# First sweep of a GLA and latent-attention layer: one float32 product in place of three float32r products, and q and k turned by VectorE and DMA

## The chip, the cores and the metric

The kernel runs on one core of one Trainium2 chip. The metric is device microseconds of one execution, taken as the median of three runs. The profile is of one more execution of the same program.

## The reference

One encoder layer over 2048 tokens of width 1024, all in float32. One input projection feeds two groups of heads, and their outputs go through one output projection, a residual and a layer norm. The change touches only the first group, a gated linear attention (GLA) with 4 heads (key width 64, value width 128), run once forwards and once backwards over chunks of tokens:

```
b = cumsum(log_a)                        # per key dimension, log_a <= 0
q_dec, k_dec = q * exp(b), k * exp(-b)
attn    = where(mask, q_dec . k_dec, 0)  # inside a chunk
o_intra = attn . v
state   = state * exp(b_last) + k_tail . v ;  o_inter = q_dec . state
o = rms_norm(o_fwd + o_bwd) * silu(gate)
```

The second group is a latent attention (MLA) with dense softmax over all 2048 keys.

## The kernel before

The program has three stages in one launch: a first sweep over 16 chunks of 128 tokens (`sweep_a`, chunk 15 down to 0, up to about 355 us of the profile), a second sweep (`sweep_c`, up to about 600 us), and the attention.

In the first sweep each chunk goes through these parts, each a generator `ga_...` of the class:

- `products`: the input projection of the chunk in three groups of columns, `ipa` tiles of PSUM. Group 0 (288 columns) holds the low-rank gates `lr` and q, group 1 (384) holds k and the first head of v, group 2 (384) the other three heads of v. Then come the gate's columns, tile `ipg` (`gate_products`, 512 columns), whose SiLU is `gate_end`, lines 1509 to 1515: three ScalarE passes and one VectorE product (`gs`). The `ipa` and `ipg` tiles share a pool of two PSUM buffers in turn: group 0 and group 2 use one, group 1 and the gate the other.
- `ga_lr`, `ga_lrT`, `ga_z`, `ga_sums`: the decay, as `E1` and `E2`, the exponentials of plus and minus the cumulated sum.
- `ga_q2`, `ga_k2`: copies q and k out of PSUM, each head's 64 columns twice side by side. `ga_q`, `ga_k`: four TensorE transposes each (`qT`, `kT`, lines 955 and 974), then times `E1` and `E2` on VectorE to `qd` and `kd`. Rows 0 to 63 of these tiles are the forward direction, rows 64 to 127 the backward one.
- `ga_kt`: `kd` transposed back (`kt`). `ga_intra`: `Ap` = k.q inside the chunk for both directions, mask, `At`. `ga_av`: `Op` = At.v. `ga_state`: `Up` = kt.v, the chunk's share of the state.

Every product of two float32 tiles is done as three float32r products of a high and a low half (`mm3`, lines 424 to 426; `hi` at line 370 makes the high half on ScalarE, `lo` at line 376 the low half on VectorE). For `Ap` the two directions stand side by side in `qbh` and `qbl`, 256 columns in which the other direction's half of the rows is zero, so that one product over 128 rows gives both. For `Op` and `Up` the high and low half of v stand side by side in `VV`, 256 columns.

The order of work: chunks 15 to 12 follow a list written out by hand (`ORDER_A`), enforced on every engine. Chunks 11 to 0 are a loop: in the step of chunk c the table `STEPS_A` puts `ga_q` and `ga_k` of the chunk before (c+1) after the fifth of the eight k-slices of group 0, `ga_kt` and `lrT` after the fifth of group 1, `z`, `cw` and `ga_intra` at the end of group 1, `ga_state` in group 2, and `ga_av` in the gate's products. Outside the hand-written list a scheduler may still move an instruction ahead where its operands are ready sooner. DMAs are issued by SyncE's queue (SP) in one order: x of a later chunk (`xaf`), and the stores of `qd`, `oi`, `Us`, `Sm` and `gs` to DRAM, which the second sweep reads. After the last chunk the weights of the second sweep (`wmr`, `wzr`) are loaded into the freed space.

Of the kernel before, what the change touches and what calls it, by code (L numbers as in the profile page):

```python
# [18 lines left out]
P = 128  # L19
# [3 lines left out]
NCH = S // P  # L23
H = 4
# [58 lines left out]
    lo=(11.99, 11.22, 11.21, 12.62, 11.98, 11.51, 10.87, 10.63),  # L83
    pv=(12.35, 12.1, 11.89, 12.65, 12.27, 12.25, 12.14, 11.45),
# [20 lines left out]
    lo=(15.35, 16.07, 20.38, 20.41, 24.45, 25.82, 33.5, 36.25),  # L105
    pv=(16.29, 16.53, 21.45, 24.62, 26.22, 30.32, 41.89, 43.83),
# [82 lines left out]
    lo=(-0.5, 0.357),  # L189
# [170 lines left out]
class K:  # L360
# [145 lines left out]
    def run(self):  # L506
        tc, nc, ins = self.tc, self.nc, self.ins
        with ExitStack() as top:
# [8 lines left out]
            self.qr_s = [[dp.tile([H, 64, QB], F32, name=f"r{p}_s{b}") for p in "hl"] for b in range(NQB)]  # L517
            self.gm_s = [dp.tile([P, H, QB], F32, name=f"gm_s{b}") for b in range(NQB)]
            self.oa_s = [dp.tile([P, H, P], F32, name=f"oa_s{c}") for c in range(NCH)]
            self.r_s = [dp.tile([1, H, QB], F32, name=f"r_s{b}") for b in range(NQB)]  # L520
            self.ob_s = [dp.tile([P, H, QB], F32, name=f"ob_s{b}") for b in range(NQB)]

# [100 lines left out]
    def sweep_a(self):  # L623
        tc, nc, ins, cp = self.tc, self.nc, self.ins, self.cp
        with ExitStack() as ctx:
# [9 lines left out]
            qbh = [wp.tile([P, H, 2, P], F32R, name=f"qbh{i}") for i in range(1)]  # L635
            qbl = [wp.tile([P, H, 2, P], F32R, name=f"qbl{i}") for i in range(1)]
# [10 lines left out]
            for t in qbh + qbl:  # L647
                nc.gpsimd.memset(t.bitcast(F32), 0.0)
            nc.vector.memset(Sb, 0.0)

            with tc.tile_pool(name="sta", bufs=1, reuse_waits="tile") as sta:
# [37 lines left out]
            cst = dict(qbh=qbh[0], qbl=qbl[0], Sb=Sb, mask=mask, rmask=rmask, wg=wg, g1=g1, tr=tr, gp=gp)  # L689
# [61 lines left out]
            with self.after(ch[i]["Ahi"]):  # L751
                self.gate_end(0, g1)
            run("state", i)
            run("av", i)
# [43 lines left out]
    def ga_k2(self, d):  # L798
        d["k2"] = d["g1"].tile([P, H, 2, 64], F32, tag="k2", name=f"k2_{d['c']}", bufs=2)
        self.hi(d["k2"], d["pt", 1][:, 0:256].rearrange("p (h o d) -> p h o d", h=H, o=1).to_broadcast([P, H, 2, 64]))  # L800
        yield

    def ga_v1(self, d):
        VV = d["VV"] = d["g1"].tile([P, H, 2, P], F32R, tag="VV", name=f"VV_{d['c']}", bufs=2)
        self.hi(VV[:, 0, 0], d["pt", 1][:, 256:384])
        yield
        self.lo(VV[:, 0, 1], d["pt", 1][:, 256:384], VV[:, 0, 0])
        yield

    def ga_v3(self, d):  # L810
        VV, pv = d["VV"], d["pt", 2][:, 0:384].rearrange("p (h d) -> p h d", h=3)
        self.hi(VV[:, 1:4, 0], pv)
        yield
        self.lo(VV[:, 1:4, 1], pv, VV[:, 1:4, 0])
        yield

    def ga_ld(self, i):
# [131 lines left out]
    def ga_q(self, d):  # L949

        nc, c = self.nc, d["c"]
        qbh, qbl = d["qbh"], d["qbl"]
        qT = d["tr"].tile([P, H, P], F32, tag="tr", name=f"qT{c}")
        for h in range(H):
            nc.tensor.transpose(qT[:, h], d["q2"][:, h].rearrange("p a d -> p (a d)"), self.ident)
        yield
        qd = self.t512(d, "qd")
# [3 lines left out]
        halves = (slice(0, 64), 0), (slice(64, 128), 1)  # L961
        for r, j in halves:
            self.hi(qbh[r, :, j], qd[r])
            yield
        for r, j in halves:
            self.lo(qbl[r, :, j], qd[r], qbh[r, :, j])
            yield

    def ga_k(self, d):

        nc, c = self.nc, d["c"]
        kT = d["tr"].tile([P, H, P], F32, tag="tr", name=f"kT{c}")
        for h in range(H):
            nc.tensor.transpose(kT[:, h], d["k2"][:, h].rearrange("p a d -> p (a d)"), self.ident)
        yield
        kd = d["kd"] = self.t512(d, "kd")
        nc.vector.tensor_tensor(kd, kT, d["E2"], ALU.mult)
        yield
        kh = d["kh"] = self.t512(d, "kh", dt=F32R)
        self.hi(kh, kd)  # L980
        yield
        kl = d["kl"] = self.t512(d, "kl", dt=F32R)
        self.lo(kl, kd, kh)
        yield

    def ga_kt(self, d):

        nc, c = self.nc, d["c"]
        kt = d["tr"].tile([P, H, P], F32, tag="tr", name=f"kt{c}")
        for h in range(H):  # L990
            nc.tensor.transpose(kt[:, h], d["kd"][:, h], self.ident)
        yield
        kth = d["kth"] = self.t512(d, "kth", dt=F32R)
        self.hi(kth, kt)
        yield
        ktl = d["ktl"] = self.t512(d, "ktl", dt=F32R)
        self.lo(ktl, kt, kth)
        yield

    def ga_intra(self, d):  # L1000

        nc, c = self.nc, d["c"]
        Ap = d["gp"].tile([P, H, 2, P], F32, tag="gp", name=f"Ap{c}")
        for h in range(H):
            self.mm3(Ap[:, h], d["kh"][:, h], d["kl"][:, h], d["qbh"][:, h], d["qbl"][:, h])
        yield
        At = self.t512(d, "At")
        nc.scalar.activation(At, Ap[:, :, 1], AF.Copy)
        yield
        nc.vector.copy_predicated(At, d["mask"][:, None, :].to_broadcast([P, H, P]), Ap[:, :, 0])  # L1010
        yield
        Ah = d["Ah"] = self.t512(d, "Ah", dt=F32R)
        d["Ahi"] = self.hi(Ah, At)
        yield
        Al = d["Al"] = self.t512(d, "Al", dt=F32R)
        self.lo(Al, At, Ah)
        yield

    def ga_av(self, d):
        nc, c = self.nc, d["c"]  # L1020
        mm = nc.tensor.matmul
        Ah, Al, VV = d["Ah"], d["Al"], d["VV"]
        Op = d["gp"].tile([P, H, 2, P], F32, tag="gp", name=f"Op{c}")
        for h in range(H):
            mm(Op[:, h], Ah[:, h], VV[:, h], start=True, stop=False)
# [4 lines left out]
        yield  # L1030
        nc.vector.tensor_tensor(oi, Op[:, :, 0], oi, ALU.add)
        self.store(c).dma_start(self.oi_s[c], oi.rearrange("p h t -> p (h t)"))
        yield

    def ga_state(self, d):

        nc, c = self.nc, d["c"]
        mm, V, G = nc.tensor.matmul, nc.vector, nc.gpsimd
        kth, ktl, VV, Sb, cw = d["kth"], d["ktl"], d["VV"], d["Sb"], self.cw[:, c]
        lo, up = slice(0, 64), slice(64, 128)  # L1040
        Up = d["gp"].tile([P, H, 2, P], F32, tag="gp", name=f"Up{c}")
        for h in range(H):
            mm(Up[:, h], kth[:, h], VV[:, h], start=True, stop=False)
            mm(Up[:, h, 0], ktl[:, h], VV[:, h, 0], start=False, stop=True)
        yield
        Us = self.t512(d, "Us")
        nc.scalar.activation(Us, Up[:, :, 1], AF.Copy)
        yield
        V.tensor_tensor(Us, Up[:, :, 0], Us, ALU.add)  # L1049
        yield  # L1050
        G.tensor_tensor(Us, Us, cw[:, 1, :, None].to_broadcast([P, H, P]), ALU.mult)  # L1051
        self.store(c).dma_start(self.su_s[c][lo], Us.rearrange("p h t -> p (h t)")[lo])
        yield
        if d["i"] > 2:
            yield from self.ga_bst(d)
        if c > 0:
            G.tensor_tensor(Sb[up], Sb[up], Us[up], ALU.add)
        yield

    def ga_bst(self, d):  # L1060
# [987 lines left out]
```

## Time and profile before

| | us |
|---|---|
| median of 3 runs (1295.48 to 1295.51) | 1295.5 |
| profiled execution, its own time | 1295.28 |
| its span in the profile | 1293.4 |
| TensorE busy in the span | 1273.7 |
| VectorE / ScalarE / GpSimd busy | 962.8 / 816.2 / 786.1 |

In a row of the timeline the columns are start, duration, engine, line, operation, output <- inputs, shapes and count. Matmuls are pipelined: a row's duration is its latency, and what it costs TensorE is the distance from its start to the start of the next row. PEld is the loading of a matmul's weights, which runs beside the matmul ahead of it. A float32 matmul that is not a transpose shows as two rows of PE and two of PEld, a float32r one as one of each. The windows give, for each stretch, the busy time of PE, PEld, VectorE (DVE), ScalarE (ACT) and GpSimd (POOL), the granted clock of TensorE, the DMA engines' busy share, and GB/s.

### The profile page before, as it was taken

The page shows a single profiled execution, that of the slowest core. Times are in us where ns is not written, and L with a number is a line of the kernel's source. Part 1 is how long each engine was busy: PE and PEld are TensorE (multiplying, and loading weights), DVE is VectorE, ACT ScalarE, POOL GpSimd, SP SyncE. Part 2 cuts the span into 40 slices and gives each one's busy share as a digit, 9 for nine tenths or more (in the row PEclk, how much of TensorE's full clock was granted, in tenths as well). Part 3 has the DMA queues.
Part 4 walks back from the last instruction along what each step waited for, and adds up shares of the span by engine and source line. Part 5 has one row for each costly group of instructions (what it writes and reads, how often), then busy time and mean ns, then how long its engine had stood idle before and what let it go on. Part 6 is the DMA issues. An engine that isn't in the chain of part 4 may idle for free.

```text
span 1293.4 us, 19959 instructions
## 1 busy us (share of the span) xinstructions
PE 1273.7 (98%) x7082; PEld 1127.9 (87%) x7082; DVE 962.8 (74%) x1706; ACT 816.2 (63%) x1334; POOL 786.1 (61%) x494
## 2 busy tenths in 40 slices
PE   8999999999999999999999999999999999999997
PEld 7999999999989999999788888888888888888886
DVE  7966675656675455554898888888888889469997
ACT  7765656566676656665688888888888888511110
POOL 0143333242458666762298888889999999944441
PEclk9999999999999999999999999999999999999999
DMA  8222313132475555665401111122223110366652
GB/s 294 66 92 56 93 53 94 50 86 62 143 261 174 194 197 179 200 208 174 128 1 41 42 42 41 42 58 63 61 72 103 46 41 9 123 214 201 214 193 98
DMA packets 105795, 145.81 MB, mean 113 GB/s; under 512 B 16630, under 2 KB 59262, under 8 KB 105696
## 3 DMA queue, kind: packets, MB, share of 16 engines
q1 hardware_dynamic: 97632, 142.41, 35.3%
q0 software_dynamic: 672, 2.10, 0.4%
q8 instruction: 56, 0.92, 0.3%
q10 hardware_dynamic: 7392, 0.03, 0.3%
q14 instruction: 43, 0.35, 0.1%
HBM read 94.14 MB, written 50.36 MB: 112 GB/s over the span
## 4 chain that ended last, share of the span: by engine, by line
PE 85%; DVE 4%; issue 2%; POOL 2%; ACT 1%; DMA 1%; SPq 0%; DVEq 0%; POOLq 0%
PE pz L1222 6%; PE ipm L1293 5%; PE o L424 4%; PE o L425 4%; PE o L426 4%; PE pS L1554 4%; PE pS L1556 4%; PE pS L1557 4%; PE pS L1555 4%; PE pS L1558 4%; PE ipa L424 4%; PE ipa L426 4%; PE ipa L425 4%; PE ipg L424 2%; PE ipg L425 2%
## 5 line engine op out<-in xcount | busy, mean ns | idle before, releaser
L376 POOL TENSOR_TENSOR pl<-s,ph 128x1024 fp32r<-128x1024 f32 x128 | 306.1, 2409 | 57.5 <-ACT ph L370 53.6
L1576 DVE TENSOR_TENSOR rm<-pS,rm 128x512 f32<-128x512 f32 x210 | 144.8, 690 | 35.8 <-ACT s L1563 30.5
L1563 ACT ACTIVATE s<-pS 128x1024 f32<-128x1024 f32 x128 | 131.3, 1026 | 61.0 <-PE pS L1558 50.8
L1600 DVE TENSOR_TENSOR s<-s,mb 128x1024 f32<-128x1024 f32 x128 | 151.2, 1213 | 9.2 <-PE mb L1594 9.0
L1051 POOL TENSOR_TENSOR Us<-Us,cw 128x512 f32<-128x512 f32 x16 | 20.0, 1247 | 226.3 <-DVE Us L1049 187.8
L370 ACT ACTIVATE ph<-s 128x1024 fp32r<-128x1024 f32 x128 | 135.1, 1057 | 17.4 <-PE o L426 16.6
L1604 ACT ACTIVATE s<-s 128x1024 f32<-128x1024 f32 x128 | 131.4, 1050 | 11.9 <-DVE s L1600 11.9
L424 PE MATMUL ipa<-wah,xah 128*128 128x384 f32 (+1 forms) x384 | 129.0, 336 | 5.4 <-ACT wah L370 5.4
L425 PE MATMUL ipa<-wal,xah 128*128 128x384 f32 (+1 forms) x384 | 124.3, 324 | 0.6 <-DVE wal L376 0.5
L426 PE MATMUL ipa<-wah,xal 128*128 128x384 f32 (+1 forms) x384 | 124.4, 324 | 0.0
L1554 PE MATMUL pS<-qh,ckvT_h 128*128 128x512 f32 x256 | 102.6, 401 | 0.8 <-DVE rm L1576 0.4
L424 PE MATMUL o<-ph,vh 128*128 128x512 f32 x256 | 101.0, 395 | 0.0
L426 PE MATMUL o<-ph,vl 128*128 128x512 f32 x256 | 99.8, 390 | 0.0
L1556 PE MATMUL pS<-qh,ckvT_l 128*128 128x512 f32 x256 | 99.8, 390 | 0.0
L1557 PE MATMUL pS<-rh,krs 128*128 128x512 f32 x256 | 99.8, 390 | 0.0
L1558 PE MATMUL pS<-rl,krs 128*128 128x512 f32 x256 | 99.7, 389 | 0.0
L1555 PE MATMUL pS<-ql,ckvT_h 128*128 128x512 f32 x256 | 99.7, 389 | 0.0
L425 PE MATMUL o<-pl,vh 128*128 128x512 f32 x256 | 99.7, 389 | 0.0
L1627 DVE TENSOR_TENSOR ap<-ap,s 128x512 f32<-128x512 f32 x120 | 83.1, 692 | 2.6 <-ACT s L1604 0.7
L376 POOL TENSOR_TENSOR ol<-of,oh 128x512 fp32r<-128x512 f32 x32 | 42.9, 1342 | 63.8 <-ACT oh L370 63.8
L424 PEld LDWEIGHTS ipa<-wah,xah 128*128 128x128 f32 x384 | 72.8, 190 | 6.6 <-ACT wah L370 5.6
L425 PEld LDWEIGHTS ipa<-wal,xah 128*128 128x128 f32 x384 | 72.8, 190 | 1.8 <-DVE wal L376 1.3
(325 smaller groups left out, 3838.8 us busy)
## 6 DMA issues: line engine op xcount, KB each, us to landing
xcf<-xT_dram SPq DMA_DIRECT2D x16, 512.0 KB, 5.6
xr<-x_dram SPq DMA_DIRECT2D x16, 512.0 KB, 5.5
out_dram<-rr SPq DMA_DIRECT2D x32, 256.0 KB, 2.1
xaf<-xT_dram SPq DMA_DIRECT2D x14, 512.0 KB, 4.2
oib<-oi_s SPq DMA_DIRECT2D x16, 256.0 KB, 4.3
qdb<-qd_s SPq DMA_DIRECT2D x16, 256.0 KB, 5.1
SU<-su_s SPq DMA_DIRECT2D x16, 256.0 KB, 4.9
ub<-u_s SPq DMA_DIRECT2D x16, 256.0 KB, 4.2
```

The lines of the kernel that those rows point to most:

```text
L370: return nc.scalar.activation(dst, src, AF.Copy).ins
L376: return e.tensor_tensor(dst, src, hi.bitcast(F32), ALU.subtract).ins
L424: mm(out, ah, bh, start=start, stop=False)
L425: mm(out, ah, bl, start=False, stop=False)
L426: mm(out, al, bh, start=False, stop=stop)
L1554: mm(ps[:, e], kh, qh, start=True, stop=False)
L1555: mm(ps[:, e], kh, ql, start=False, stop=False)
L1556: mm(ps[:, e], kl, qh, start=False, stop=False)
L1557: mm(ps[:, e], kr, rh, start=False, stop=False)
L1558: mm(ps[:, e], kr, rl, start=False, stop=True)
L1576: V.tensor_tensor(d["rm"], src[:, e], d["rm"], ALU.max)
L1600: V.tensor_tensor(s, s, d["mb"][:, None, :].to_broadcast([P, 2, QB]), ALU.subtract)
```

## The change

It has two parts, both in the first sweep.

For all 16 chunks the high and low halves behind `Ap`, `Op` and `Up` go. Each is a plain float32 product, on `qd`, `kd`, `At`, `kt` and `V` as they are. `Ap` becomes eight products over 64 rows each, by turns over rows 0 to 63 and 64 to 127, and the two directions go to different PSUM banks (`Ap` is now `[P, 2, H, P]`). `Us` is scaled straight out of PSUM by VectorE instead of by GpSimd.

For chunks 11 to 0 (steps i from 4 to 15) `ga_q2`/`ga_k2` and the TensorE transposes go. `turn` lets VectorE transpose q (or k) within 32x32 blocks, and four DMAs from SP write it to a DRAM tile in whole transposed order, in runs of 32 float32 (128 bytes). `turned` reads it back with two DMAs, once into rows 0 to 63 and once into rows 64 to 127. `qx` follows group 0; `ql` (the reading of q) and `kx` follow group 1; `kl` (the reading of k) follows group 2.

```
+    def turn(self, d, n, src):
+        t = d["g1"].tile([P, H, 2, 32], F32, tag=f"{n}x", name=f"{n}x_{d['c']}")
+        self.nc.vector.transpose(t.rearrange("p h a t -> p (h a t)"), src)
+        dst = self.qk_s["qk".index(n)][d["c"]].rearrange("(a r) h (b t) -> b r h a t", a=2, b=4)
+        for b in range(4):
+            self.nc.sync.dma_start(dst[b], t[32 * b:32 * b + 32])
+
+    def turned(self, d, n):
+        t = d[f"{n}T"] = self.t512(d, f"{n}2", bufs=2)
+        for r in (slice(0, 64), slice(64, 128)):
+            self.nc.sync.dma_start(t[r], self.qk_s["qk".index(n)][d["c"]])
...
-            for n in ((("lr", "q2"), ("k2", "v1"), ("v3",)) if i else (("lr",), ("q2", "k2", "v1"), ("v3",)))[g]:
+            for n in ((("lr", "qx"), ("ql", "kx", "v1"), ("kl", "v3")) if i else (("lr",), ("q2", "k2", "v1"), ("v3",)))[g]:
...
     def ga_q(self, d):
-        for h in range(H):
-            nc.tensor.transpose(qT[:, h], d["q2"][:, h].rearrange("p a d -> p (a d)"), self.ident)
+        qT = d.get("qT")
+        if qT is None:
...
-        for r, j in halves:
-            self.hi(qbh[r, :, j], qd[r])
-        for r, j in halves:
-            self.lo(qbl[r, :, j], qd[r], qbh[r, :, j])
...
     def ga_k(self, d):
-        kh = d["kh"] = self.t512(d, "kh", dt=F32R)
-        self.hi(kh, kd)
-        kl = d["kl"] = self.t512(d, "kl", dt=F32R)
-        self.lo(kl, kd, kh)
...
     def ga_kt(self, d):
-        self.hi(kth, kt)
-        self.lo(ktl, kt, kth)
+        d["kt"] = self.t512(d, "kt")
+        self.hi(d["kt"], kt)
...
     def ga_intra(self, d):
-        Ap = d["gp"].tile([P, H, 2, P], F32, tag="gp", name=f"Ap{c}")
+        Ap = d["gp"].tile([P, 2, H, P], F32, tag="gp", name=f"Ap{c}")
         for h in range(H):
-            self.mm3(Ap[:, h], d["kh"][:, h], d["kl"][:, h], d["qbh"][:, h], d["qbl"][:, h])
+            for j, r in enumerate((slice(0, 64), slice(64, 128))):
+                nc.tensor.matmul(Ap[:, j, h], d["kd"][r, h], d["qd"][r, h], start=True, stop=True)
...
-        d["Ahi"] = self.hi(Ah, At)
-        self.lo(Al, At, Ah)
...
     def ga_av(self, d):
-            mm(Op[:, h], Ah[:, h], VV[:, h], start=True, stop=False)
-            mm(Op[:, h, 0], Al[:, h], VV[:, h, 0], start=False, stop=True)
+            nc.tensor.matmul(Op[:, h], d["At"][:, h], d["V"][:, h], start=True, stop=True)
-        nc.scalar.activation(oi, Op[:, :, 1], AF.Copy)
-        nc.vector.tensor_tensor(oi, Op[:, :, 0], oi, ALU.add)
+        nc.scalar.activation(oi, Op, AF.Copy)
...
     def ga_state(self, d):
-            mm(Up[:, h], kth[:, h], VV[:, h], start=True, stop=False)
-            mm(Up[:, h, 0], ktl[:, h], VV[:, h, 0], start=False, stop=True)
+            nc.tensor.matmul(Up[:, h], d["kt"][:, h], d["V"][:, h], start=True, stop=True)
-        nc.scalar.activation(Us, Up[:, :, 1], AF.Copy)
-        V.tensor_tensor(Us, Up[:, :, 0], Us, ALU.add)
-        G.tensor_tensor(Us, Us, cw[:, 1, :, None].to_broadcast([P, H, P]), ALU.mult)
+        nc.vector.tensor_tensor(Us, Up, cw[:, 1, :, None].to_broadcast([P, H, P]), ALU.mult)
```

`ga_v1` and `ga_v3` lose their low halves (`VV` becomes `V`, float32), and the tiles `qbh` and `qbl` with their memsets go.

More of the change, by code (lines that the diff above doesn't have):

```diff
@@ L519, in run @@
             self.oa_s = [dp.tile([P, H, P], F32, name=f"oa_s{c}") for c in range(NCH)]
+            self.qk_s = [[dp.tile([64, H, P], F32, name=f"{n}_s{c}") for c in range(NCH)] for n in ("qx", "kx")]
             self.r_s = [dp.tile([1, H, QB], F32, name=f"r_s{b}") for b in range(NQB)]
@@ L634, in sweep_a @@
             lrs = [wp.tile([P, 98], F32R, name=f"lr{i}") for i in range(2)]
-            qbh = [wp.tile([P, H, 2, P], F32R, name=f"qbh{i}") for i in range(1)]
-            qbl = [wp.tile([P, H, 2, P], F32R, name=f"qbl{i}") for i in range(1)]
             Sb = wp.tile([P, H, P], F32, name="Sb")
@@ L646, in sweep_a @@
                 nc.vector.memset(t[:, 96:98].bitcast(F32), 1.0)
-            for t in qbh + qbl:
-                nc.gpsimd.memset(t.bitcast(F32), 0.0)
             nc.vector.memset(Sb, 0.0)
@@ L687, in sweep_a @@
             g1 = ctx.enter_context(tc.tile_pool(name="g1", bufs=1))
-            cst = dict(qbh=qbh[0], qbl=qbl[0], Sb=Sb, mask=mask, rmask=rmask, wg=wg, g1=g1, tr=tr, gp=gp)
+            cst = dict(Sb=Sb, mask=mask, rmask=rmask, wg=wg, g1=g1, tr=tr, gp=gp)
             rope = self.rope_angles(pos_i, pos_f, invf, hpi)
@@ L750, in sweep_a @@
             run("intra", i)
-            with self.after(ch[i]["Ahi"]):
+            with self.after(ch[i]["Aset"]):
                 self.gate_end(0, g1)
@@ L801, in ga_k2, with ga_qx, ga_kx, ga_ql @@
         yield
+    def turn(self, d, n, src):
[8 more added lines that the diff above has]
+            self.nc.sync.dma_start(t[r], self.qk_s["qk".index(n)][d["c"]])
+    def ga_qx(self, d):
+        self.turn(d, "q", d["pt", 0][:, 32:288])
+        yield
+    def ga_kx(self, d):
+        self.turn(d, "k", d["pt", 1][:, 0:256])
+        yield
+    def ga_ql(self, d):
+        self.turned(d, "q")
+        yield
+    def ga_kl(self, d):
+        self.turned(d, "k")
+        yield
     def ga_v1(self, d):
[L804 to L807, printed above, removed]
+        d["V"] = self.t512(d, "V", bufs=2)
+        self.hi(d["V"][:, 0], d["pt", 1][:, 256:384])
         yield
     def ga_v3(self, d):
[L811 to L814, printed above, removed]
+        self.hi(d["V"][:, 1:4], d["pt", 2][:, 0:384].rearrange("p (h d) -> p h d", h=3))
         yield
@@ L951, in ga_q @@
         nc, c = self.nc, d["c"]
-        qbh, qbl = d["qbh"], d["qbl"]
-        qT = d["tr"].tile([P, H, P], F32, tag="tr", name=f"qT{c}")
-        for h in range(H):
-            nc.tensor.transpose(qT[:, h], d["q2"][:, h].rearrange("p a d -> p (a d)"), self.ident)
-        yield
-        qd = self.t512(d, "qd")
+        qT = d.get("qT")
+        if qT is None:
+            qT = d["tr"].tile([P, H, P], F32, tag="tr", name=f"qT{c}")
+            for h in range(H):
+                nc.tensor.transpose(qT[:, h], d["q2"][:, h].rearrange("p a d -> p (a d)"), self.ident)
+            yield
+        qd = d["qd"] = self.t512(d, "qd")
         nc.vector.scalar_tensor_tensor(qd, qT, 0.125, d["E1"], ALU.mult, ALU.mult)
@@ L960, in ga_q @@
         yield
-        halves = (slice(0, 64), 0), (slice(64, 128), 1)
-        for r, j in halves:
-            self.hi(qbh[r, :, j], qd[r])
-            yield
-        for r, j in halves:
-            self.lo(qbl[r, :, j], qd[r], qbh[r, :, j])
-            yield
     def ga_k(self, d):
         nc, c = self.nc, d["c"]
[L972 to L975, printed above, removed]
+        kT = d.get("kT")
+        if kT is None:
+            kT = d["tr"].tile([P, H, P], F32, tag="tr", name=f"kT{c}")
+            for h in range(H):
+                nc.tensor.transpose(kT[:, h], d["k2"][:, h].rearrange("p a d -> p (a d)"), self.ident)
+            yield
         kd = d["kd"] = self.t512(d, "kd")
         nc.vector.tensor_tensor(kd, kT, d["E2"], ALU.mult)
-        yield
-        kh = d["kh"] = self.t512(d, "kh", dt=F32R)
-        self.hi(kh, kd)
-        yield
-        kl = d["kl"] = self.t512(d, "kl", dt=F32R)
-        self.lo(kl, kd, kh)
         yield
@@ L992, in ga_kt @@
         yield
-        kth = d["kth"] = self.t512(d, "kth", dt=F32R)
-        self.hi(kth, kt)
-        yield
-        ktl = d["ktl"] = self.t512(d, "ktl", dt=F32R)
-        self.lo(ktl, kt, kth)
+        d["kt"] = self.t512(d, "kt")
+        self.hi(d["kt"], kt)
         yield
@@ L1020, in ga_av @@
         nc, c = self.nc, d["c"]
[L1021 to L1023 removed]
+        Op = d["gp"].tile([P, 2, H, P], F32, tag="gp", name=f"Op{c}")[:, 0]
         for h in range(H):
[L1025 to L1026 removed]
+            nc.tensor.matmul(Op[:, h], d["At"][:, h], d["V"][:, h], start=True, stop=True)
         yield
         oi = self.t512(d, "oi", bufs=2)
[L1029 to L1031 removed]
+        nc.scalar.activation(oi, Op, AF.Copy)
         self.store(c).dma_start(self.oi_s[c], oi.rearrange("p h t -> p (h t)"))
@@ L1037, in ga_state @@
         nc, c = self.nc, d["c"]
-        mm, V, G = nc.tensor.matmul, nc.vector, nc.gpsimd
-        kth, ktl, VV, Sb, cw = d["kth"], d["ktl"], d["VV"], d["Sb"], self.cw[:, c]
+        Sb, cw = d["Sb"], self.cw[:, c]
         lo, up = slice(0, 64), slice(64, 128)
-        Up = d["gp"].tile([P, H, 2, P], F32, tag="gp", name=f"Up{c}")
+        Up = d["gp"].tile([P, 2, H, P], F32, tag="gp", name=f"Up{c}")[:, 0]
         for h in range(H):
-            mm(Up[:, h], kth[:, h], VV[:, h], start=True, stop=False)
-            mm(Up[:, h, 0], ktl[:, h], VV[:, h, 0], start=False, stop=True)
+            nc.tensor.matmul(Up[:, h], d["kt"][:, h], d["V"][:, h], start=True, stop=True)
         yield
         Us = self.t512(d, "Us")
-        nc.scalar.activation(Us, Up[:, :, 1], AF.Copy)
+        nc.vector.tensor_tensor(Us, Up, cw[:, 1, :, None].to_broadcast([P, H, P]), ALU.mult)
+        self.store(c).dma_start(self.su_s[c][lo], Us.rearrange("p h t -> p (h t)")[lo])
         yield
-        V.tensor_tensor(Us, Up[:, :, 0], Us, ALU.add)
         yield
-        G.tensor_tensor(Us, Us, cw[:, 1, :, None].to_broadcast([P, H, P]), ALU.mult)
-        self.store(c).dma_start(self.su_s[c][lo], Us.rearrange("p h t -> p (h t)")[lo])
         yield
@@ L1056, in ga_state @@
         if c > 0:
-            G.tensor_tensor(Sb[up], Sb[up], Us[up], ALU.add)
+            nc.gpsimd.tensor_tensor(Sb[up], Sb[up], Us[up], ALU.add)
         yield
```

10 lines of the change are left out of this document (3 added, 7 removed).

## The prediction

> **What bounds the kernel now.** I read the page's busy shares first, then the windows, then who waited for whom on TensorE inside the first sweep, and then one step of a chunk row by row.
>
> ```profile
> span 1293.4 us, 19959 instructions
> PE 1273.7 (98%) x7082; PEld 1127.9 (87%) x7082; DVE 962.8 (74%) x1706; ACT 816.2 (63%) x1334; POOL 786.1 (61%) x494
> ...
> 150.00:200.00 50.00, 50.00 (x324) 47.78 (x323) 30.89 (x56) 30.60 (x59) 18.37 (x13) 1.00 0.27 74
> ...
> PE Up L1044 <- DVE ktl L376: 0.4, 1, 0.4
> ...
> PE Ap L426 <- DVE kl L376: 0.3, 1, 0.3
> ...
> PE Op L1025 <- ACT Ah L370: 0.4, 1, 0.4
> ```
>
> TensorE is busy in 50.00 of these 50 us at a granted clock of 1.00, VectorE in 30.89, ScalarE in 30.60, GpSimd in 18.37; DMA takes 0.27. The three waits of TensorE that have to do with this change come to 1.1 us over 16 chunks. So what is taken from VectorE, ScalarE and GpSimd in the first sweep is worth those 1.1 us at most, what is taken from TensorE counts, and the new DMAs cost nothing until TensorE waits for them. The later stages keep their instructions; they start earlier or later with the sweep.
>
> One step in the timeline, with the places that change:
>
> ```profile
> 239.11 0.39 PE L426 MATMUL ipg<-wgh,xal 128*128 128x512 f32 x1
> 239.34 0.29 PE L424 MATMUL ipa<-wah,xah 128*128 128x288 f32 x1
> 239.47 0.29 PE L425 MATMUL ipa<-wal,xah 128*128 128x288 f32 x1
> ...
> 241.31 0.60 PE L955 MATMUL qT<-ident,q 128*128 128x128 f32 x4
> 241.75 0.60 PE L974 MATMUL kT<-ident,k 128*128 128x128 f32 x4
> 242.10 0.38 PE L424 MATMUL ipa<-wah,xah 128*128 128x288 f32 x1
> 242.32 0.29 PE L425 MATMUL ipa<-wal,xah 128*128 128x288 f32 x1
> ...
> 243.38 0.35 PE L424 MATMUL ipa<-wah,xah 128*128 128x384 f32 x1
> ```
>
> **Transposes of q and k.** From the first qT (241.31) to the second projection row behind kT (242.32) is 1.01 us; two projection rows stand 0.13 us apart, so the eight transposes cost 0.88 us of TensorE. They go in 12 chunks: **-10.6 us**.
>
> **What is late next.** In the changed program as built, `kt` no longer waits for the middle of group 1: two of its four transposes stand ahead of group 1, and group 1 has to wait until VectorE has read the gate out of the same PSUM buffer (`gs`). That chain:
>
> ```profile
> 239.31 1.06 ACT L370 ACTIVATE xah<-xaf 128x1024 fp32r<-128x1024 f32 x1 [1.98 <-PE ipg L425]
> 240.28 0.58 ACT L1509 ACTIVATE gs<-ipg 128x512 f32<-128x512 f32 x1
> ...
> 241.56 0.63 ACT L1513 ACTIVATE gs<-gs 128x512 f32<-128x512 f32 x1
> ...
> 242.56 0.68 DVE L1515 TENSOR_TENSOR gs<-ipg,gs 128x512 f32<-128x512 f32 x1
> ...
> 223.79 0.60 PE L991 MATMUL kt<-ident,kd 128*128 128x128 f32 x4
> 224.22 0.27 PE L891 MATMUL lrT<-ident,lr 128*98 128x128 f32 x1
> ```
>
> Today `gs` ends at 243.24 and group 1 starts at 243.38, unhindered. ScalarE keeps xah and its three passes in this order, so `gs` can start at 242.25 at the earliest (ScalarE ends at 242.19) and end at 242.93; with 0.1 us allowed for the hand-over, group 1 may start at about 243.03. TensorE would be there at 243.38 - 0.88 + 0.3 (two transposes of `kt`, 0.43/2, and the change into and out of them) = 242.80. So 0.2 us of the 0.88 turn into a wait, and the moved half of `kt` gives back 0.22 of its 0.3. That is 0.28 us in each of 11 steps (chunk 0 has no step behind it): **+3.1 us**; bounds 0, if the silu chain gets that much earlier too, and +6.3, if group 1 keeps today's 0.14 us behind `gs` and nothing of `kt` is given back.
>
> **The float32 products.** The trace has one plain float32 product, `pabs` of the second sweep: eight products of 128x128x128, 16 rows.
>
> ```profile
> 372.43 1.95 PE L1186 MATMUL pabs<-wkr,wqT 128*128 128x128 f32 x16
> 374.13 0.36 PE L1222 MATMUL pz<-xch,wzh 128*128 128x256 f32 x1
> 374.33 0.28 PE L1222 MATMUL pz<-xcl,wzh 128*128 128x256 f32 x1
> ...
> 372.23 1.96 PEld L1186 LDWEIGHTS pabs<-wkr,wqT 128*128 128x128 f32 x16
> 374.10 0.19 PEld L1222 LDWEIGHTS pz<-xch,wzh 128*128 128x128 f32 x1
> ...
> 226.32 0.33 PE L424 MATMUL Ap<-qbh,kh 128*128 128x256 f32 x1
> ...
> 227.78 0.35 PE L424 MATMUL ipa<-wah,xah 128*128 128x384 f32 x1
> ...
> 229.89 0.28 PE L1043 MATMUL Up<-VV,kth 128*128 128x256 f32 x1
> ...
> 230.75 0.39 PE L424 MATMUL ipa<-wah,xah 128*128 128x384 f32 x1
> ...
> 235.68 0.28 PE L1025 MATMUL Op<-VV,Ah 128*128 128x256 f32 x1
> ...
> 236.53 0.45 PE L424 MATMUL ipg<-wgh,xah 128*128 128x512 f32 x1
> ```
>
> Eight take 1.70 us by the matmuls (372.43 to 374.13) and 1.87 by the weight loads (372.23 to 374.10): 0.21 to 0.23 us each. `Up` now takes 0.86 us, `Op` 0.85; four float32 products each are 0.85 to 0.94. Taken at +0.01 for each of 32: **+0.3 us** (bounds 0 and +2.7).
>
> `Ap` now takes 1.46 us (226.32 to 227.78). The new eight products have 64 rows each, by turns in the lower and the upper half of the array, from disjoint partitions into different banks. No row of this trace has a product over half the rows. If they run one behind the other they cost what `pabs` costs, up to 1.87 us; if each two run side by side, half of 1.70, 0.85. Neither row is nearer, and a partial overlap (weights loaded one after the other, products side by side) lies between; I take the middle, 1.35 us: -0.11 in 16 chunks, **-1.8 us** (bounds -9.8 and +6.6). The Trainium skill says two things here. TensorE: Matmul & The Clock Gate, Part 3, has matmuls in different row groups start about 4 ns apart, which would give the lower bound. TensorEngine Tiling (Array Packing), Key Properties, says "Changing tiling mode (not just tile) drains the TensorE", which speaks against the change; no row here can show either.
>
> **Waits and the end of the sweep.** The three waits above go with `kl`, `ktl` and `Ah`: **-1.1 us** (bounds -1.1 and 0). In chunk 0 no gate of a next step covers the way of k: from the end of group 1 to `kt` there are only group 2, `Op` and 18 gate products; I put **+0.5 us** there (0 to 1). Behind it the splitting of the second sweep's weights on VectorE loses the low halves queued ahead of it, so it is not later than today.
>
> **VectorE, ScalarE, GpSimd** lose the halves, and GpSimd the scaling of `Us`, which VectorE does in place of an addition of the same shape. VectorE gains two block transposes of 128x256, an operation that the trace lacks; between the split of 128x128 and a product of 128x512:
>
> ```profile
> 226.92 0.29 DVE L376 TENSOR_TENSOR VV<-ipa,VV 128x128 fp32r<-128x128 f32 x1 [1.18 <-ACT VV L370]
> ...
> 234.26 0.68 DVE L1049 TENSOR_TENSOR Us<-Up,Us 128x512 f32<-128x512 f32 x1
> ```
>
> 0.29 to 0.68 us each, 0.45 taken; hidden, as VectorE is idle 19 of 50 us.
>
> **The way through DRAM.** Twelve DMAs more in each step on SP. Rows:
>
> ```profile
> 220.69 0.34 SPq L490 DMA_DIRECT2D xaf<-xT_dram  x1
> ...
> 221.59 0.38 SPq L855 DMA_DIRECT2D u_s<-gs  x1
> 236.19 0.45 SPq L1052 DMA_DIRECT2D su_s<-Us  x1
> ...
> 225.93 0.56 PE L903 MATMUL z<-lrTs,wg 98*128 98x128 f32 x4
> ...
> gm_s<-gm SPq DMA_DIRECT2D x8, 512.0 KB, 3.6
> oa_s<-oT SPq DMA_DIRECT2D x16, 256.0 KB, 2.1
> su_s<-Us SPq DMA_DIRECT2D x14, 128.0 KB, 2.2
> ```
>
> SP issues two in 0.90 us (220.69 to 221.59, one row between) and is free from 222 to 236. One q or k is 4 x 256 runs of 128 bytes, 64 packets on each of 16 engines. The nearest price: `gm_s` is 512 runs of 1 KB (32 an engine) and lands in 3.6 us, `oa_s` is 128 runs of 2 KB (8 an engine) in 2.1: 1.5/24 = 62 ns a packet, which a shorter run should not exceed; the lower end is nothing beyond the 2.1.
> At 62 ns, in the clock of the step above (k leaves PSUM from 225.93, `kt` comes at the end of the next group 0, 242.5): q's writes queue behind the loads and stores issued from 220.7 on and land by 230. SP issues the first write of k at 226.9, then waits at the reading of q until 230 and so keeps the other three writes of k waiting; these go out until 232.3 and land by 237. The reading of k waits for them; its second half stands behind the store of `Us`, ready at 234.9. Issued by 238, landed by 241 (2.2 in the row of `su_s`, 3 allowed), `kd` (0.68, as `gs`) done by 241.7. That is 0.8 us ahead of `kt`, and at half the price 3 us or more. So **0 us** on TensorE; behind this wait on VectorE stand `gs` and the next `lr` and `qx`, which would then be late too.
>
> **Sum** against the profiled execution (1295.28 us; span 1293.4 and 1.9 around it; the median of the runs is 0.2 above): -10.6 + 3.1 + 0.3 - 1.8 - 1.1 + 0.5 = -9.6, so 1285.7, and on the scale of the median **1286 us**. With `Ap` fully side by side 1278; with `Ap` at 1.65 us 1291: the forecast's own range, chance 0.6.
>
> **Rivals.** *The 64-row products run singly* (0.22): `Ap` at 1.87 gives 1294. If the array has to run empty at each change between 128 and 64 rows, it costs the end of a row that is otherwise overlapped, 0.27 us long less the 0.11 at which transposes follow each other, twice in 16 chunks: +5, and 1299 (0.06 of the 0.22; this is the rule of TensorEngine Tiling in the Trainium skill). For it: the weight loads of `pabs` are as dense as its matmuls, so nothing is left to overlap if loads stay in one line. Against it: the halves share neither partitions nor banks. A measurement of this kernel tells 0.2% from no change, 2.6 us (1292.9 to 1298.1), so most of this rival is "same".
>
> *The way through DRAM comes late* (0.13), slower. Place: `kd` on VectorE, ahead of `kt` and `gs`. It decides from about 70 ns a packet: 64 packets of q and 48 of k stand in one line, so 7 ns more use up the 0.8 us. At 90 ns `kt` waits (112 x 28 ns) - 0.8 = 2.3 us in 11 steps, +25.6, and the time is 1311; at 80 ns 1299. For it: no store in the trace has runs this short. The Trainium skill (DMA: Bandwidth & Descriptors, Specifications) says that below 512 B a write becomes a read-modify-write; no run here shows it. Against it: the sweep's DMA share is 0.27.
>
> A remainder (0.05) is for a cost not seen, above all in the hand-ordered chunks 15 to 12 and at the change to the second sweep. That the change doesn't do what it says is no case: the eight transposes are TensorE rows that go.
>
> **Chances and range.** Faster 0.6 + 0.03 of the single products = 0.63; same 0.13 (singly, without the array running empty); slower 0.24 (the rest). 1277 to 1301 leaves out some 0.05 below and, above, the DRAM case beyond 80 ns and part of the remainder, some 0.13.
>
> **What would show it.** In the changed profile: no `qT`, `kT` after 100 us; group 1 waiting some 0.2 us for `gs` in each step; `Ap` from first row to next `ipa` 0.85 to 1.87 us; `kd` ending before group 0 does; TensorE's share of the windows still full. Wrong if TensorE waits for `kd` in every step (the DRAM way), if `Ap` takes more than 1.9 us, or if the stretch behind 355 us grows.

## The result, and the profile after

| | before, us | after, us |
|---|---|---|
| median (5 runs each) | 1295.51 | 1288.98 |
| range of the runs | 1295.48 to 1296.32 | 1288.48 to 1290.23 |
| span of the profile | 1293.4 | 1287.2 |

The ratio is 0.9947, with a 95% interval of 0.9936 to 0.9958: 6.5 us faster, where 9.5 were forecast. From the page of the changed kernel, the window of the sweep that the prediction showed, and the three longest of the waits of TensorE that are new (us in total, times, longest):

```profile
PE 1262.9 (98%) x7050; PEld 1110.6 (86%) x7050; DVE 912.8 (71%) x1602; ACT 755.5 (59%) x1230; POOL 765.9 (60%) x476
...
150.00:200.00 50.00, 49.60 (x321) 46.27 (x321) 25.69 (x42) 19.54 (x43) 14.43 (x9) 1.00 0.44 114
...
PE ipm L1287 <- DVE xcl L376: 1.4, 1, 1.4
PE kt L1002 <- DVE kd L994: 1.2, 1, 1.2
PE pS L1548 <- ACT s L1557: 1.0, 1, 1.0
```

TensorE lost 10.8 us of work (1273.7 to 1262.9) and the span 6.2. In the window TensorE is no longer full (49.60 of 50.00) and DMA has gone from 0.27 to 0.44. None of the three waits stood in the trace of before.

One step of the sweep, TensorE's timeline of the changed kernel (start, duration, line, operation, count):

```profile
215.44 0.29 PE L426 MATMUL ipa<-wah,xal 128*128 128x288 f32 x1
215.57 0.38 PE L1002 MATMUL kt<-ident,kd 128*128 128x128 f32 x2
216.08 0.45 PE L424 MATMUL ipa<-wah,xah 128*128 128x384 f32 x1
216.37 0.34 PE L425 MATMUL ipa<-wal,xah 128*128 128x384 f32 x1
...
218.82 0.38 PE L1002 MATMUL kt<-ident,kd 128*128 128x128 f32 x2
219.04 0.27 PE L912 MATMUL lrT<-ident,lr 128*98 128x128 f32 x1
...
220.73 0.56 PE L924 MATMUL z<-lrTs,wg 98*128 98x128 f32 x4
221.22 1.16 PE L1014 MATMUL Ap<-qd,kd 64*128 64x128 f32 x16
222.31 0.44 PE L424 MATMUL ipa<-wah,xah 128*128 128x384 f32 x1
222.59 0.33 PE L425 MATMUL ipa<-wal,xah 128*128 128x384 f32 x1
...
240.53 0.27 PE L912 MATMUL lrT<-ident,lr 128*98 128x128 f32 x1
```

From `lrT` to `lrT` a step is 21.49 us (219.04 to 240.53), where before's are mostly 22.21 to 22.24: some 0.70 us in each step. Of the eleven steps of chunks 10 to 0, nine lie at 21.46 to 21.52; the two from 262.05 to 306.53 take 22.21 and 22.27, and before they took 24.90 and 20.26. Between 215.44 and 222.59 no `qT` or `kT` is left; the two halves of `kt` stand at 215.57 and 218.82; `Ap` takes 1.09 us to the start of the next row.

The sweep's lead was 9.3 us when the second sweep began (first `ipm` at 358.23 instead of 367.56), 7.7 us at its first `pz` (366.44 instead of 374.13), 6.4 us at the last `pS` of the attention (1081.29 instead of 1087.68). So the sum of -9.6 was right up to the end of the first sweep, though by errors that cancel (see below), and some 3 us were given back behind it.

### The profile page after: what moved, and what is told of

It is laid out like the page before. It is cut to its first block, busy times and chain, and to the rows that moved or that the text cites. A ratio compares the mean times of both kernels' runs of the same rounds, so it can differ in the third digit from the quotient of the medians.

```text
span 1287.2 us, 19847 instructions
## 1 busy us (share of the span) xinstructions
PE 1262.9 (98%) x7050; PEld 1110.6 (86%) x7050; DVE 912.8 (71%) x1602; ACT 755.5 (59%) x1230; POOL 765.9 (60%) x476
## 4 chain that ended last, share of the span: by engine, by line
PE 81%; DMA 5%; DVE 4%; ACT 3%; issue 3%; POOL 2%; SPq 2%; DVEq 0%; ACTq 0%; POOLq 0%
PE pz L1216 6%; PE ipm L1287 5%; PE o L424 4%; PE o L425 4%; PE o L426 4%; PE pS L1548 4%; PE pS L1550 4%; PE pS L1551 4%; PE pS L1552 4%; PE pS L1549 4%; PE ipa L424 4%; PE ipa L426 3%; PE ipa L425 3%; PE ipg L425 2%; PE ipg L424 2%
## 5 line engine op out<-in xcount | busy, mean ns | idle before, releaser
L1051 POOL TENSOR_TENSOR Sb<-Sb,Us 64x512 f32<-64x512 f32 x15 | 21.5, 1434 | 188.0 <-ACT E L961 133.7
```

## The experiments

All were compared with the kernel before, which stood at 1296.0 us beside `f32_only`, `turn_only`, `ap_by_half` and `xah_late` and at 1295.28 us beside the other four. Each trace is of one run. For `split_late` (1296.19 us), `ap_by_half` (1298.58) and `xah_late` (1290.93) that run is 1.7 to 3 us above the median given here.

### Each half of the change alone

*Float32 products alone* (`f32_only`): q and k are turned by TensorE in all chunks, as before.

```
-            for n in ((("lr", "qx"), ("ql", "kx", "v1"), ("kl", "v3")) if i else (("lr",), ("q2", "k2", "v1"), ("v3",)))[g]:
+            for n in ((("lr", "q2"), ("k2", "v1"), ("v3",)) if i else (("lr",), ("q2", "k2", "v1"), ("v3",)))[g]:
```

> Only the float32 products; q and k of every chunk are still transposed by TensorE. Theory (both parts pay, the products by the pairs of 64 rows): a step between two lrT transposes shrinks by 0.37 us in Ap less 0.2 for the two changes of 64 and 128 rows, and 0.05 in Up and Op, so 0.2 of 22.2 us in each step, some 3.5 us over 16 chunks and up to 1 us of waits: 1291 to 1292.5. Rival (the products are worth nothing, all of the gain is the transposes): 1295.5 within 1 us.

Measured: 1293.27 us, ratio 0.998 [0.9971, 0.9989], so 2.7 us less than before, and 0.8 us outside the range that I expected. Its steps are 22.04 to 22.08 us, on average 0.15 less than before. At the first `ipm` it is 3.75 us ahead of before (363.81 instead of 367.56), at the first `pz` 2.7 (371.41 instead of 374.13): between them TensorE waits 0.8 us for `xcl`, a wait that comes back in the changed kernel.

*Turning through DRAM alone* (`turn_only`): the products stay split in halves, and `Us` stays with GpSimd. What the kernel keeps of before:

```
         Ap = d["gp"].tile([P, H, 2, P], F32, tag="gp", name=f"Ap{c}")
         for h in range(H):
             self.mm3(Ap[:, h], d["kh"][:, h], d["kl"][:, h], d["qbh"][:, h], d["qbl"][:, h])
```

> Only the turning of q and k by VectorE and DMA in chunks 11 to 0; the products stay three float32r products. Theory: a step loses the eight transposes (0.88 us) and gets back 0.4 of it around kt and the start of group 1, which waits for gs: 21.7 instead of 22.2 us a step, 12 steps, less some 1 to 2 us at the change to the second sweep: 1290.5 to 1292. Rival (the transposes are worth all of the gain): 1289. Rival (the DRAM way alone costs more than it brings, since kd and its halves now stand on VectorE ahead of gs): 1295 or more.

Measured: 1350.04 us, ratio 1.042 [1.0406, 1.0435]. My expectation was wrong by over 50 us. The second rival has the direction, and its reason (`kd` and its halves stand on VectorE ahead of `gs`) points at the order of work; its first words blame the way through DRAM. The trace tells the two apart. TensorE's largest wait, then one step on ScalarE, VectorE, SP and TensorE:

```profile
PE ipa L424 <- DVE gs L1549: 41.2, 11, 4.2
...
239.09 1.28 ACT L370 ACTIVATE qbh<-qd 64x512 fp32r<-64x512 f32 x2 [0.97 <-DVE qd L990]
244.43 0.63 ACT L370 ACTIVATE kh<-kd 128x512 fp32r<-128x512 f32 x1 [4.06 <-DVE kd L1011]
...
245.44 1.05 ACT L370 ACTIVATE xah<-xaf 128x1024 fp32r<-128x1024 f32 x1
...
240.69 2.98 DVE L376 TENSOR_TENSOR qbl<-qd,qbh 64x512 fp32r<-64x512 f32 x2
243.70 0.69 DVE L1011 TENSOR_TENSOR kd<-k,E 128x512 f32<-128x512 f32 x1
...
234.80 1.12 SPq L815 DMA_DIRECT2D k<-kx_s  x2
...
249.08 0.44 PE L424 MATMUL ipa<-wah,xah 128*128 128x384 f32 x1 [4.13 <-DVE gs L1549]
```

k's reading went out at 234.80, nine microseconds before `kd`, and `kd` has no wait in brackets behind it: it is late because VectorE does two `qbl` first, which take 2.98 us. On ScalarE `kh` waits 4.06 us for `kd`, and behind `kh` are queued `xah` and the gate's passes, which in the kernel before stood ahead of it. So `gs`, and with it group 1, comes four microseconds late. If this reading holds, the cause is the order on VectorE and ScalarE and not the DRAM way.

*The same with the splitting put behind the gate* (`split_late`): one edit against `turn_only`.

```
     def ga_kt(self, d):
...
             nc.tensor.transpose(kt[:, h], d["kd"][:, h], self.ident)
         yield
+        if d["i"] > 3:
+            with self.after(*self.gs_done):
+                for _ in self.split_q(d):
+                    pass
+                for _ in self.split_k(d):
+                    pass
```

(`split_q` and `split_k` are the four lines each that make `qbh`, `qbl`, `kh`, `kl`; they leave `ga_q` and `ga_k`. `gs_done` is the gate's last ScalarE pass and its VectorE product.)

> The kernel with the turning through DRAM and float32r products (the one of 1350 us), with one change: from chunk 4 of the order on, the splitting of qd and kd in halves (qbh, kh on ScalarE, qbl, kl on VectorE) is put behind the gate's activations and gs of the step, not ahead of them. Theory: the way through DRAM is in time there too, and the 4.2 us that TensorE waited for gs in each step came of kh standing ahead of xah and the gate on ScalarE, and kd behind two qbl of 1.5 us on VectorE; then the steps fall from 26 to 21.5 to 22.0 us and the time to 1288 to 1293 us. Rival: q and k through DRAM take VectorE and SP so much time with the halves there that kd is late wherever the halves stand: steps above 23.5 us and a time above 1310.

Measured: 1293.24 us, ratio 0.9987 [0.9976, 0.9998]. The steps are mostly 21.66 us, in the range of the theory and 0.55 below before; the time is 0.24 us above its range. The 57 us between the two kernels are shown to be the place of the splitting; what its part on ScalarE and its part on VectorE cost apart is not. Two places keep it from gaining more. One is the step from 286.23 to 310.89, which takes 24.66 us with two waits of TensorE, 1.01 for `kd` and 0.76 for `gs`. The other is chunk 0, where the splitting still stands ahead:

```profile
345.10 3.14 DVE L376 TENSOR_TENSOR qbl<-qd,qbh 64x512 fp32r<-64x512 f32 x2 [0.23 <-ACT qbh L370]
...
349.61 1.12 PE L1037 MATMUL kt<-ident,kd 128*128 128x128 f32 x4 [2.91 <-DVE kd L1017]
```

With this wait of 2.91 us the granted clock falls, and is 0.50 from 349 to 355.

In the steps the two halves of the change add up: -0.15 (products) and -0.55 (turning), against -0.70 together.

### The 64-row products

*`Ap` by halves* (`ap_by_half`): the changed kernel, with the four products of rows 0 to 63 first and those of rows 64 to 127 behind them, not by turns.

```
-        for h in range(H):
-            for j, r in enumerate((slice(0, 64), slice(64, 128))):
+        for j, r in enumerate((slice(0, 64), slice(64, 128))):
+            for h in range(H):
```

> The changed kernel, with the eight 64-row products of Ap in another order: four in the lower half of the array, then four in the upper half, instead of by turns. Theory (two products in different halves run side by side): Ap goes from 1.09 us to the price of products one behind the other, 1.7 to 1.9 us, +0.6 to +0.8 in 16 chunks, 1298 to 1301. Rival (64-row products are cheaper by themselves, by their fewer rows): Ap stays at 1.1 us and the time at 1289.

Measured: 1296.78 us, ratio 1.0004 [0.9995, 1.0013], 7.8 us above the changed kernel by the medians and 7.4 by the ratios; I had expected at least 1298. TensorE's timeline:

```profile
226.41 1.71 PE L1014 MATMUL Ap<-qd,kd 64*128 64x128 f32 x16
228.04 0.44 PE L424 MATMUL ipa<-wah,xah 128*128 128x384 f32 x1
```

1.63 us to the next row, where the turns take 1.09. In 16 chunks 0.54 us are 8.6 us. By turns the trace's rows start in pairs, 7 ns apart within a pair and 0.11 us from pair to pair; by halves most of them start singly, 0.11 us apart, and only a few around the change of half pair up. So products over different halves of the rows run side by side where they stand next to each other in the order: the same 16 rows, the same operands. The order of two loops is worth about as much as the whole change brought.

### The wait of group 1 for the gate

*`xah` late* (`xah_late`): the changed kernel, with the splitting of the next x on ScalarE put behind the gate's three passes.

```
-        self.hi(xh[:, :, 0], xf)
+        with self.after(*([self.gs_act] if i > 4 else [])):
+            self.hi(xh[:, :, 0], xf)
```

> The changed kernel, with the high half of the next x (xah, 1.06 us on ScalarE) put behind the three SiLU passes instead of ahead of them. Theory (group 1 waits for the SiLU chain): gs ends 1 us earlier, group 1 follows group 0 without a wait, a step falls from 21.5 to about 21.1 us and the time by 11 x 0.4 = 4.4 to about 1284.6, less what the second sweep's DMAs hold back. Rival (TensorE is held by kt, which waits for kd from DRAM): no change of the step, 1289.

Measured: 1289.22 us, ratio 0.9948 [0.9935, 0.996]: nothing gained over the change. Yet the steps are 21.11 us, 0.39 less, as expected. One step loses it again. TensorE's timeline at its two ends, a wait, VectorE, and the window from the end of that wait to the end of the step (the last three columns are granted clock, DMA share, GB/s):

```profile
280.70 0.32 PE L913 MATMUL lrT<-ident,lr 128*98 128x128 f32 x1 [0.25 <-DVE lr L376]
...
307.37 0.42 PE L913 MATMUL lrT<-ident,lr 128*98 128x128 f32 x1
...
PE ipa L424 <- DVE gs L1510: 3.4, 1, 3.4
...
299.48 1.42 DVE L995 TENSOR_TENSOR kd<-k,E 128x512 f32<-128x512 f32 x1 [7.51 <-DMA k<-kx_s]
300.82 0.68 DVE L1510 TENSOR_TENSOR gs<-ipg,gs 128x512 f32<-128x512 f32 x1
...
301.56:307.37 5.81, 5.81 (x19) 5.71 (x20) 0.39 (x2) 0.00 (x0) 0.00 (x0) 0.50 0.63 158
```

The step from 280.70 to 307.37 takes 26.67 us instead of after's 22.27. There k's reading went out at 294.11, behind two stores of the step and a load of x in SP's order, and came after 299.4; behind `kd` stands `gs`. TensorE waits 3.43 us for it, and at a granted clock of 0.50 the 5.81 us behind the wait cost some 2.9 more. This is the DRAM rival's place, in one step of twelve; the late start of the reading comes of SP's order.

*Sf cleared by GpSimd* (`sf_pool`): the changed kernel, with one instruction on another engine.

```
-            self.nc.vector.memset(Sf, 0.0)
+            self.nc.gpsimd.memset(Sf, 0.0)
```

The reason, from the changed kernel's VectorE and TensorE timelines at the end of the sweep:

```profile
355.93 0.48 DVE L1117 MEMSET Sf<- 64x512 f32 x1 [3.14 <-DMA oi_s<-oi]
...
358.90 2.35 DVE L376 TENSOR_TENSOR xcl<-xcf,xch 128x1024 fp32r<-128x1024 f32 x2
...
360.17 0.47 PE L1287 MATMUL ipm<-wmh,xcl 128*128 128x448 f32 x1 [1.38 <-DVE xcl L376]
```

> The changed kernel with one instruction moved: Sf, the tile of the second sweep's state, is set to zero by GpSimd instead of VectorE. Theory: in the changed kernel the clearing of Sf waits for the store of oi, which lands late in the stretch with full DMA engines behind 340 us, and VectorE's splitting of xcl behind it makes TensorE wait 1.4 us ahead of ipm. With the clearing off VectorE that wait goes: 1287.6 us (1287.0 to 1288.3). Rival: the transfers of that stretch themselves come 1.4 us too late, since the first sweep now ends earlier; then TensorE waits as long for the next of them, and the time stays at 1289.

Measured: 1286.7 us, ratio 0.9928 [0.9916, 0.9941]. The first `pz` comes 1.0 us earlier than in the changed kernel (365.4), and the wait of `ipm` is gone. From the first `ipm` to the first `pz` TensorE takes 6.57 us, as before, where the changed kernel takes 8.21. The first `ipm` itself comes 0.6 us later (358.82), since in this run `kt` of chunk 0 waits 0.61 us for `kd`. By the medians the gain over the changed kernel is 2.3 us, where 1.4 was expected, and the time lies just below the range that I gave. The runs (1285.14 to 1287.26) lie below all of the changed kernel's, so the rival, 1289, is out; whether the gain is 1.4 or 2.3 they don't tell.

*Both* (`best`): `xah` late in steps 5 to 12 only, and Sf on GpSimd.

```
+        with self.after(*([self.gs_act] if 4 < i < 13 else [])):
...
+            self.nc.gpsimd.memset(Sf, 0.0)
```

> The changed kernel with two edits: in steps 5 to 12 the splitting of the next x (xah, ScalarE) goes behind the gate's three activations, and Sf is cleared by GpSimd. Theory: the wait of group 1 for gs costs 0.39 us a step, as the steps of 21.11 instead of 21.50 us in the kernel with xah late in all steps show, and that kernel lost its gain only in one later step, at k's reading behind the stores of the step. Without that step: 8 x 0.39 = 3.1 and 1.4 from Sf, 1284.5 us (1283.5 to 1286). Rival: whatever the steps gain is given back before the second sweep, since the end of the first sweep waits for transfers: 1288 to 1289.

Measured: 1282.72 us, ratio 0.9911 [0.9897, 0.9924]: 12.6 us below before and some 6 below the changed kernel, and lower than the range of the theory. It is clear of `xah_late`; against `sf_pool` the intervals overlap. Seven steps, from the `lrT` at 89.72 to the one at 237.53, take 21.11 or 21.12 us each, and the first `ipm` comes at 354.95.

### How much the DRAM way has to spare

*Each short write twice* (`twice`): a second tile in DRAM takes a copy that nothing reads.

```
+            self.nc.sync.dma_start(twin[b], t[32 * b:32 * b + 32])
             self.nc.sync.dma_start(dst[b], t[32 * b:32 * b + 32])
```

> The changed kernel, with each of the 96 writes of 128-byte runs (qx_s, kx_s) also sent to a second place in DRAM that nothing reads, ahead of the real one: twice the short packets and twice the issues on SP. Theory: kd is 3.3 us ahead of kt in the changed kernel, and the writes cost what SP takes to issue them (0.64 us each, 5.1 us more a step), so k's reading goes out 4 to 5 us later, kd comes 1 to 2 us too late for kt, and 12 steps cost 12 to 25 us: 1301 to 1314. By the 62 ns a packet of the prediction (64 packets more for q and for k on each engine, 8 us) it would be above 1335. Rival: the slack is larger than it looks, and the time stays below 1292.

Measured: 1310.71 us, ratio 1.012 [1.0106, 1.0133]. TensorE's waits, and in one step SP's queue and VectorE:

```profile
PE kt L1005 <- DVE kd L997: 13.9, 8, 3.0
PE ipm L1290 <- DVE xcl L376: 5.9, 1, 5.9
...
215.59 0.61 SPq L809 DMA_DIRECT2D kx_s<-kx  x1
...
220.90 0.33 SPq L984 DMA_DIRECT2D qd_s<-qd  x1
...
221.81 1.12 SPq L814 DMA_DIRECT2D k<-kx_s  x2
...
225.28 0.69 DVE L997 TENSOR_TENSOR kd<-k,E 128x512 f32<-128x512 f32 x1 [4.40 <-DMA k<-kx_s]
```

`kt` now waits for `kd`, 1.7 us in each of eight steps, 13.9 together, within the 12 to 25 that the theory gave for this place. The other large part is at the change to the second sweep, where `ipm` waits 5.9 us for `xcl` (1.4 in the changed kernel). A write holds SP for 0.61 us. But the last of them goes out at 215.59 and k's reading only at 221.81: with the writes later, the store of `qd` has come to stand ahead of the reading in SP's queue (220.90), and it waits for VectorE. So the theory's mechanism, issues that push the reading back, is only half of it; the other half is what the reading then stands behind. The 62 ns a packet of the prediction would have made the time above 1335 us; the measured time is far below.

## Why the prediction was right or wrong

**The likeliest case came in, at 1289.0 instead of 1286.0.** By its terms:

- *Transposes*, -0.88 us a step: no `qT` or `kT` row is left. Right.
- *Group 1 behind `gs`*, +0.28 a step: the changed kernel shows 0.93 us from 215.44 to 216.37, with half of `kt` and the wait in it; without them three such rows stand 0.13 and 0.17 us apart, so 0.63 is theirs; the other half takes 0.22 less than all of `kt` did. That makes +0.40, and `xah_late` takes 0.39 of it away. The mechanism was right; the term was 0.12 a step too small, 1.3 us over 11 steps.
- *`Ap`*, -0.11 a chunk: the eight products take 1.09 us and run side by side, near the lower bound of 0.85. But the way in is 0.49 us (`z` to `Ap`, 0.39 before), and the second row behind comes 0.28 us after the first (222.31 to 222.59), where 0.18 was usual: 0.1 us at each end. Together about -0.17. The middle of 1.35 was right within 0.06 by luck: it isn't a partial overlap. The rows start in pairs 7 ns apart, eight pairs at 0.11 us are 0.89, and the two ends cost the rest: the first pair stands 0.21 us ahead of the second, the last 0.20 ahead of the next row. `Up`, float32 over all 128 rows, has 0.11 and 0.03 there, so each change of rows costs some 0.2 us. Of the two rules of the Trainium skill weighed there, TensorE: Matmul & The Clock Gate, Part 3, is what the trace shows (7 ns, where it says about 4). TensorEngine Tiling (Array Packing), Key Properties, on the drain at a change of mode, agrees with it in kind, at these 0.2 us a change where I took 0.16.
- *All products with their waits*, +0.3 - 1.8 - 1.1 = -2.6: `f32_only` measured -2.7, but not by these terms. It is 3.75 us ahead at the end of the sweep and gives 1.0 back at `xcl`, a loss that the sum lacked. And of the three waits one stayed: in chunk 0 `Op` waits 0.57 us for `At`, where it waited 0.4 for `Ah`. The changed kernel's row:

```profile
347.00 1.16 PE L1026 MATMUL Op<-V,At 128*128 128x128 f32 x8 [0.57 <-DVE At L1019]
```

- *The sweep as a whole*: of its 9.3 us the products are 3.75, where 2.6 stood in the sum, and the turning is the other 5.6, where -10.6 + 3.1 + 0.5 = -7.0 stood. That the whole came within 0.3 us of the sum is luck.
- *The DRAM way*, 0: TensorE waited for `kd` in one step of twelve. The changed kernel's SP and VectorE, in the step shown:

```profile
216.96 2.65 SPq L806 DMA_DIRECT2D qx_s<-qx  x4
...
224.35 1.91 SPq L806 DMA_DIRECT2D kx_s<-kx  x3
...
232.40 1.40 DVE L994 TENSOR_TENSOR kd<-k,E 128x512 f32<-128x512 f32 x1
```

`kd` ends at 233.8 and the next `kt` starts at 237.09: 3.3 us to spare, where I had 0.8. The price per packet was too high, as `twice` shows; most of the time here is SP's issuing, which the prediction took from long rows (two in 0.90 us) and which is some 0.65 us for each of these writes. So the threshold of that rival, 70 ns a packet, stood on the wrong quantity.

**The step that failed** is "Behind it the splitting of the second sweep's weights on VectorE loses the low halves queued ahead of it, so it is not later than today". VectorE had less queued, but ahead of the splitting stands the clearing of Sf, which waits 3.14 us for the store of `oi` (355.93, above). In the kernel before VectorE came to it later, and it had no wait:

```profile
364.71 0.48 DVE L1123 MEMSET Sf<- 64x512 f32 x1
```

TensorE waits 1.4 us for `xcl`, and `sf_pool` takes that wait away: from the first `ipm` to the first `pz` are 6.57 us before, 8.21 in the changed kernel and 6.57 in `sf_pool`. The wait comes with the products: it stands in `f32_only` and not in `split_late`. I had looked at the engine's queue and not at what its instructions wait for. The prediction had named a longer stretch behind 355 us as a sign of being wrong, and that stretch is 3 us longer. Inside the sweep 1.2 us went in one step near the end, where `kt` waited for `kd`. The term for chunk 0's end, +0.5, was some 0.9 too high: from the last `lrT` to the first `ipm` TensorE takes 30.2 us, 1.4 less than before, where about -0.5 was forecast. And some 1.3 us went between the first `pz` and the last `pS`, with a wait of `pS` for `s` of 1.0 us that before didn't have. Why that wait appears was not tried, and that loss stays open.

**The rivals.** *64-row products run singly*: refuted by the 1.09 us of the changed kernel. `ap_by_half` comes near that case and stands at 1296.8 (I had 1294 without and 1299 with the draining). *The DRAM way late*: it cost 1.2 us in one step of the change, and the same place, `kd` ahead of `kt` and `gs`, decides in `twice` and in one step of `xah_late`; each time through what k's reading stands behind on SP.

## What to carry to other kernels

Before a step is moved off the bound engine, follow the chain that ends just behind it: here 0.88 us left TensorE and 0.40 came back at once, because the next buffer is freed by ScalarE and VectorE, and moving one instruction on ScalarE was worth 0.39 a step. An engine that is only half busy can still ruin a step through its order: half the change alone cost 54 us since the splitting of `qd` and `kd` stood ahead of the gate. And ask of every instruction ahead of a stage's first product what it waits for, not only how much is queued.

## What the runs showed of the hardware

**VectorE waits for GpSimd when both its operands lie in SBUF.** `kd` and `qd` now read both operands from SBUF. VectorE and GpSimd in the changed kernel:

```profile
230.82 1.53 DVE L980 SCALAR_TENSOR_TENSOR qd<-q,E 128x512 f32<-128x512 f32 x1
...
230.69 1.11 POOL L1066 TENSOR_TENSOR Sm<-Sb,cw 64x512 f32<-64x512 f32 x1
231.88 1.37 POOL L1070 TENSOR_TENSOR Sb<-Sb,cw 64x512 f32<-64x512 f32 x1
```

and in the kernel with `xah` late, where GpSimd has just ended:

```profile
228.91 1.37 POOL L1071 TENSOR_TENSOR Sb<-Sb,cw 64x512 f32<-64x512 f32 x1
...
230.29 0.69 DVE L995 TENSOR_TENSOR kd<-k,E 128x512 f32<-128x512 f32 x1 [0.91 <-DMA k<-kx_s]
```

The same `kd` took 1.40 us beside GpSimd's work (232.40) and 0.69 us without it; `qd` 1.53 us. This is not half speed: `qd` ends 0.55 us behind `Sm` (231.80, 232.35) and `kd` 0.55 us behind `Sb` (233.25, 233.80). Of the 24 `qd` and `kd` with both operands in SBUF in the changed kernel, 20 took 0.81 to 2.29 us, and each of them ended 0.54 to 0.56 us behind a GpSimd operation; the other four took 0.68 or 0.69. So VectorE seems to wait until the GpSimd operation is over. Before, with one operand in PSUM, `qd` took 0.69 us while GpSimd was splitting x:

```profile
240.51 2.39 POOL L376 TENSOR_TENSOR xal<-xaf,xah 128x1024 fp32r<-128x1024 f32 x1 [0.66 <-ACT xah L370]
...
241.95 0.69 DVE L958 SCALAR_TENSOR_TENSOR qd<-qT,E 128x512 f32<-128x512 f32 x1 [3.89 <-PE qT L955]
```

The Trainium skill (GPSIMD Engine Reference, Specifications) says that the SBUF interfaces are shared and that VectorE instructions with two SBUF inputs contend with GpSimd; these rows agree. The same contention shows in `turn_only`, where two `qbl` take 2.98 us, and before 1.40 (243.75).

**A wait can cost TensorE half its clock behind it.** In `turn_only`, windows of 1 us behind the wait of 4.13 us that ends at 249.08 (the last three columns are granted clock, DMA share, GB/s):

```profile
249.00:250.00 1.00, 0.92 (x5) 0.93 (x6) 0.48 (x3) 0.00 (x0) 0.00 (x0) 1.00 0.14 12
250.00:251.00 1.00, 1.00 (x5) 1.00 (x4) 0.00 (x0) 0.00 (x0) 0.00 (x0) 0.50 1.22 119
...
252.00:253.00 1.00, 1.00 (x4) 1.00 (x4) 0.00 (x0) 0.00 (x0) 0.00 (x0) 0.50 0.99 378
253.00:254.00 1.00, 1.00 (x7) 0.91 (x7) 0.00 (x0) 0.22 (x1) 0.00 (x0) 0.80 1.00 197
```

From 250 on the granted clock is 0.50 for some 3.4 us, which costs some 1.7 us more. Together 5.8 us, and this step, from the `lrT` at 226.32 to the one at 253.58, takes 27.26 us where `split_late` takes 21.66: here the wait is charged 1.4 times. The Trainium skill (TensorE: Matmul & The Clock Gate, Part 1) puts the array at half its clock after about 3.4 us of idleness. The rows agree on the half, but not on a fixed length: the clock fell to 0.50 with a wait of 2.91 us in `split_late` and one of 1.81 us in `twice` (154.19), and stayed at 1.00 behind one of 2.85 us in `turn_only` (356.83).
